# Nine mixer buffers for seven in a two-layer diffusion step, and an output projection that closes over attention

## The chip, the cores and the metric

The kernel runs on one core of a Trainium2 chip. A core has five engines with a queue of instructions each: PE (TensorE, matrix products; its weight loads are shown as PEld), DVE (VectorE), ACT (ScalarE), POOL (GpSimd) and SP (SyncE, which here only issues transfers). Each engine takes its instructions in the order in which they stand in its queue. The metric is the device time of one execution in microseconds (us).

## The reference

One inference step of a backbone with two layers of one form, each with its own weights. 128 context rows and 512 latent rows (640 in all) of width 1024 go through, per layer:

```python
hn = rmsnorm(x, norm_w[0]) * (1.0 + scale1) + shift1
z = hn @ w_in                               # 1024 -> 9 * 256
q, k, v, gb, gc, xb, xr, gr, xp = jnp.split(z, 9, axis=-1)
y_a = diff_attn(q, k, v, ...)               # 4 heads; softmax - lam * softmax, then a norm per head
y_b = gb * depthwise_conv(gc * xb, conv_b_w)
y_c = (hf + hb) * gelu(gr)                  # hf, hb: RG-LRU of conv(xr), forward and backward
y_d = pool_mixer(xp, pool_w, pool_scale)
x = x + gate1 * (concatenate([y_a, y_b, y_c, y_d]) @ w_out)
hn = rmsnorm(x, norm_w[1]) * (1.0 + scale2) + shift2
x = x + gate2 * (square(relu(hn @ w_mlp1)) @ w_mlp2)
```

The shifts, scales and gates come from a product of a conditioning vector with `w_ada`. All is float32.

## The kernel before

**Layout.** Activations lie transposed: the 1024 features are 8 chunks of 128 partitions, the 640 rows are columns, in two halves A and B of 320. To keep float32's precision, each operand is split into a high part (rounded to fp32r) and a low part (the rest), and a product is three matmuls: high x high, low x high, high x low. A result tile of 128 features by 320 columns over 8 chunks is thus a group of 24 matmuls of 320 columns. Weights come by transfers into five staging buffers `st`; ACT makes the high half `wh` (L276), DVE the low half `wl` (L259). `whl` has four buffers of each.

**Who sets the order.** The program is written down by Python generators. The main line writes the matmul groups; each call of `tick` lets every waiting helper (`rope_gen`, `attn_gen`, `rg_gen`, `gelu_gen`, `pool_gen`, `convb_gen`) write its next piece and lets the weight stream take a step. `until` calls `tick` again and again until a condition holds, a free buffer for instance. A scheduler then orders each engine's instructions by the place at which they were written down and by when their operands are there in its own model. What comes out is a fixed queue for each engine.

**The mixer stage of a layer.** The main line does `q`, `k`, then (`ORD`) `v`, `xr`, `gc`, `xb`, `xp`, `gr`, `gb`. Evacuated projections lie in the mixer buffers `m` (`NM` of them, 664 columns each, used round robin); helpers take temporaries from `z` and `m`. Output chunk pairs of the mixer are y0, y1 (attention), y2, y3 (short convolution, made from `gb`), y4, y5 (RG-LRU with gelu), y6, y7 (pooling).

- Attention unit: scores into `S` (L1022, PE), maximum (L1031, DVE), two exponentials (L1035, ACT), their combination `e` (L1042, DVE), transposes (L1049, L1054, PE), copies to `pt` (L1056, L1057, ACT), product with values (L1069, PE), copy to `osb` (L1074, DVE).
- Attention's closing, after its last unit: squares (L1110, ACT), sums per head (L1113, PE), scale `fin` (L1116 DVE, L1118 root on ACT, L1120 reciprocal on DVE); then for f = 0 and 1: spread over columns (L1131, DVE), five transposes into `TA` and `TB` (L1135, PE; one buffer each), scaled product (L1138, DVE), high part (L1139, ACT), low part (L1140, DVE). That is y0 and y1.
- RG-LRU: gates (L1177 PE, L1181 ACT), roots (L1199), products (L1202, L1203), scans (L1210), sums (L1212, L1218). Gelu and gate: L1231 to L1242, split at L866 and L868. Pooling: L1259 to L1275, product L1288 (PE), split L1290 (ACT) and L1291 (DVE). Convolution's last step: L1373 (DVE), L1376 (ACT), L1379 (DVE).

**The output projection's opening** (`gemm_early`, L799) holds four result tiles open in four PSUM banks (two of `g`, two of `S`). It first adds the chunks named in `EARLY`, then waits until all mixer outputs have been written down and no helper is left, then adds the others (`late`) and evacuates each tile into the residual (L1443, DVE). Before, the early chunks are y0, y1, y6, y4, y2, y3 (18 matmuls a tile), the late ones y5 and y7 (6 a tile). After these four tiles the projection goes on with 24 matmuls a tile (L778). Beside it run parts of the `w_ada` product on DVE and ACT (L501, L499) and the next norm's squares (L691, L694, L697).

Of the kernel before, what the change touches and what calls it, by code (L numbers as in the profile page):

```python
# [24 lines left out]
DEPTH = 2  # L25
EPS = 1e-6
GP = 664
NM = 7
OFF = 120
OFFW = 120  # L30
OFFO = 0
OFFT = 60
EARLY = (0, 1, 6, 4, 2, 3)
ORD = ("v", "xr", "gc", "xb", "xp", "gr", "gb")
QH = (0,)
BT = (1, 2)
# [82 lines left out]
class Net:  # L119
    def __init__(self, tc, es, ins, outs, consts):  # L120
# [14 lines left out]
        self.z = Slots(sl, [f"z{i}" for i in range(16)], [P, XC])  # L135
        self.m = Slots(sl, [f"m{i}" for i in range(NM)], [P, GP])
        self.e = Slots(sl, [f"e{i}" for i in range(3)], [P, T])
# [1177 lines left out]
    def layer(self, l, last):  # L1315
# [157 lines left out]

        self.gemm_early(seq[:4], mov_y, evo, EARLY, [k for k in range(KT) if k not in EARLY], gate)
        self.gemm(seq[4:], mov_y, evo,
# [399 lines left out]
```

## Time and profile before

| | |
|---|---|
| time, median of 3 runs | 1445.24 us (1445.22 to 1445.91) |
| the profiled execution | 1442.92 us, its span 1441.1 us |
| PE busy | 1416.9 us, 98% of the span |
| DVE, ACT, POOL busy | 1028.0, 728.4, 61.9 us |
| mean granted clock of PE | 0.994 |

Busy time of PE counts the matmuls' modelled ends, which overlap: a 320-column matmul is listed with 0.31 us, while the next starts 0.147 us later. Start times say more there. On DVE and ACT too, the next instruction starts a little before the listed end of the one before it.

### The profile page before, as it was taken

The numbers are of one execution on the slowest core, as the hardware profiler recorded it, in microseconds if no ns is written. First come the engines' busy times: TensorE is split into PE (matmuls) and PEld (weight loads), VectorE is DVE, ScalarE is ACT, GpSimd is POOL, SyncE is SP. The second block draws the span as 40 slices with busy tenths as digits, with TensorE's granted clock in tenths as the row PEclk, the third lists the DMA queues.
The fourth block names the chain that finished last, engine by engine and source line by source line (L and its number), as shares of the span: only waits on it lengthen the run. The fifth ranks groups of instructions, "written<-read, shape, count | busy, mean of one in ns | idle before, by whom it ended". The sixth has DMA issues, their size and how long they took to land.

```text
span 1441.1 us, 24506 instructions
## 1 busy us (share of the span) xinstructions
PE 1416.9 (98%) x9703; PEld 1345.6 (93%) x9703; DVE 1028.0 (71%) x1938; ACT 728.4 (51%) x1377; POOL 61.9 (4%) x105
## 2 busy tenths in 40 slices
PE   7999999999999999999999999999999999999998
PEld 6877989999999999999999999999999999999997
DVE  4566889896968769588968778998384644644753
ACT  5534795365347237237445577636532722722731
POOL 1122000010000000000102200000000000000000
PEclk8999999999999999999999999999999999999999
DMA  9686214435245635446634401262232432432401
GB/s 330 204 223 182 81 35 94 158 118 178 90 146 176 190 114 170 156 148 199 197 102 129 129 30 59 45 191 74 88 102 76 145 103 77 143 103 79 142 15 73
DMA packets 154970, 183.45 MB, mean 127 GB/s; under 512 B 10788, under 2 KB 130040, under 8 KB 154856
## 3 DMA queue, kind: packets, MB, share of 16 engines
q1 hardware_dynamic: 150264, 175.29, 39.7%
q0 software_dynamic: 4224, 6.45, 2.0%
q8 instruction: 76, 1.25, 0.4%
q14 instruction: 38, 0.31, 0.1%
q10 hardware_dynamic: 368, 0.16, 0.0%
HBM read 169.28 MB, written 3.15 MB: 120 GB/s over the span
## 4 chain that ended last, share of the span: by engine, by line
PE 82%; DVE 8%; DMA 6%; ACT 2%; issue 1%; POOL 0%; DVEq 0%; ACTq 0%
PE g_L_0A L778 9%; PE g_L_1A L778 9%; PE g_L_1B L778 9%; PE g_L_0B L778 9%; PE S L443 9%; PE f L443 5%; DMA st<-in_w_mlp 2%; DMA st<-in_w_ada 2%; PE g_L_v L1405 2%; PE g_L_o_0B L778 1%; PE g_L_o_1B L778 1%; PE g_L_o_1A L778 1%; PE g_L_o_0A L778 1%; PE TB L443 1%; PE TB L1069 1%; DVE wl L259 1%
## 5 line engine op out<-in xcount | busy, mean ns | idle before, releaser
L259 DVE TENSOR_TENSOR wl<-st,wh 128x1024 fp32r<-128x1024 f32 x212 | 258.3, 1221 | 104.1 <-ACT wh L321 55.4
L276 ACT CAST wh<-st 128x1024 fp32r<-128x1024 f32 x132 | 138.4, 1049 | 126.7 <-PE g_L_1B L778 85.0
L321 ACT CAST wh<-st 128x1024 fp32r<-128x1024 f32 x84 | 88.1, 1049 | 136.1 <-PE g_L_1B L778 94.9
L778 PE MATMUL g_L_0A<-z,wh 128*128 128x320 f32 (+1 forms) x512 | 124.2, 315 | 0.0
L778 PE MATMUL g_L_1A<-z,wh 128*128 128x320 f32 (+1 forms) x512 | 121.6, 314 | 0.0
L778 PE MATMUL g_L_0B<-z,wh 128*128 128x320 f32 (+1 forms) x512 | 116.5, 307 | 0.0
L778 PE MATMUL g_L_1B<-z,wh 128*128 128x320 f32 (+1 forms) x512 | 116.2, 307 | 0.0
L778 PEld LDWEIGHTS g_L_0A<-z,wh 128*128 128x128 f32 x512 | 88.2, 188 | 2.2 <-ACT z L418 2.0
L778 PEld LDWEIGHTS g_L_1A<-z,wh 128*128 128x128 f32 x512 | 87.6, 188 | 0.8 <-issue 0.8
L778 PEld LDWEIGHTS g_L_0B<-z,wh 128*128 128x128 f32 x512 | 86.2, 188 | 1.7 <-DVE x L1443 1.7
L778 PEld LDWEIGHTS g_L_1B<-z,wh 128*128 128x128 f32 x512 | 86.4, 188 | 0.9 <-issue 0.8
L501 DVE SCALAR_TENSOR_TENSOR pt<-st,SC,pt 128x512 f32<-128x512 f32 x112 | 79.7, 744 | 10.1 <-ACT pt L499 5.4
L501 DVE SCALAR_TENSOR_TENSOR m<-st,SC,m 128x512 f32<-128x512 f32 x112 | 78.8, 744 | 7.4 <-DMA st<-in_w_ada 5.5
L778 PE MATMUL g_L_0A<-z,wl 128*128 128x320 f32 (+1 forms) x256 | 79.9, 312 | 0.0
L778 PE MATMUL g_L_1A<-z,wl 128*128 128x320 f32 (+1 forms) x256 | 79.8, 312 | 0.0
L778 PE MATMUL g_L_1B<-z,wl 128*128 128x320 f32 (+1 forms) x256 | 78.6, 307 | 0.0
L778 PE MATMUL g_L_0B<-z,wl 128*128 128x320 f32 (+1 forms) x256 | 78.3, 306 | 0.0
L694 ACT ACTIVATE e<-x 128x320 f32<-128x320 f32 (+2 forms) x56 | 26.3, 470 | 102.8 <-DVE x L1443 102.7
L318 DVE TENSOR_TENSOR st<-st,st 128x1024 f32<-128x1024 f32 x48 | 58.5, 1220 | 27.0 <-DMA st<-in_w_mlp 26.9
L443 PE MATMUL S<-hh,wh 128*128 128x320 f32 x192 | 61.8, 322 | 3.6 <-DVE e L461 3.2
L1031 DVE TENSOR_REDUCE mx<-S 128x2 f32<-128x1280 f32 x32 | 47.5, 1486 | 20.2 <-PE S L1022 20.0
L443 PE MATMUL S<-hh,wl 128*128 128x320 f32 x192 | 59.3, 309 | 0.0
(682 smaller groups left out, 4205.5 us busy)
## 6 DMA issues: line engine op xcount, KB each, us to landing
st<-in_w_mlp SPq DMA_DIRECT2D x164, 512.0 KB
st<-in_w_ada SPq DMA_DIRECT2D x80, 512.0 KB
st<-in_w_in SPq DMA_DIRECT2D x36, 512.0 KB
st<-in_w_out SPq DMA_DIRECT2D x16, 512.0 KB
z<-in_w_ada SPq DMA_DIRECT2D x24, 256.0 KB
z<-qk SPq DMA_DIRECT2D x32, 80.0 KB
z<-qk POOLq DMA_DIRECT2D x32, 80.0 KB, 4.0
xt<-in_x_sample SPq DMA_DIRECT2D x4, 512.0 KB
```

Of the source, the lines that this page charges most:

```text
L259: eng.tensor_tensor(wl.rearrange("p k c -> p (k c)"), st, wh.bitcast(F32).rearrange("p k c -> p (k c)"), OP.subtract)
L276: nc.scalar.copy(wh.rearrange("p k c -> p (k c)"), st)
L318: nc.vector.tensor_tensor(st, st, self.held[add][0], OP.add)
L321: nc.scalar.copy(wh.rearrange("p k c -> p (k c)"), st)
L443: nc.tensor.matmul(bank[mi][:, 0:HC], w[:, k, sl], x, start=(fresh and n == 0), stop=(n == 11), skip_group_check=not fresh)
L501: nc.vector.scalar_tensor_tensor(acc[:, 0:512], w, col, acc[:, 0:512], OP.mult, OP.add)
L694: nc.scalar.activation(s[:, 0:n], self.x[:, k, cs], AF.Square)
L778: nc.tensor.matmul(pt[:, 0:ncols], w[:, k % 4, sl], r, start=(n == 0), stop=(n == 23))
L1031: nc.vector.tensor_reduce(mx[:, 0:2], ps[:, 128:1408].rearrange("p (s k) -> p s k", s=2), AX.X, OP.max)
L1069: nc.tensor.matmul(tb[64 * j:64 * j + 64, 0:P], self.vsb[:, kt, (h - 1 + j) * 64:(h + j) * 64], self.pTs[j][:, kt * P:(kt + 1) * P], start ...
L1405: nc.tensor.matmul(pt[:, 0:256], a[:, k, ts], b[:, k % 4, :], start=(n == 0), stop=(n == 23))
```

## The change

Three constants. `NM`: nine buffers `m0` to `m8` for seven. `EARLY`: four chunks for six, in another order; the late ones are now y0, y1 (attention), y5 and y7, so the four tiles have 12 early and 12 late matmuls each. The scratch in which POOL's transfers are prepared shrinks from 8192 to 4096 bytes per partition.

```diff
-NM = 7
+NM = 9
...
-EARLY = (0, 1, 6, 4, 2, 3)
+EARLY = (2, 6, 4, 3)
...
-    nc = bacc.Bacc("TRN2", target_bir_lowering=False, num_devices=1, dynamic_dma_scratch_size=8192)
+    nc = bacc.Bacc("TRN2", target_bir_lowering=False, num_devices=1, dynamic_dma_scratch_size=4096)
```

Every engine has the same instructions as before. Their order differs in two stretches, one per layer: from about the `gc`/`xb` groups to the first tiles of the output projection. Outside of them it is the same but for a handful of swaps.

On PE in layer 0, before, the second group of attention's closing transposes (`TA_2536`, of `e_49`) stands among the matmuls of `gb`:

```order
L778 MATMUL g_L_gb_0B<-hh,wh_2211 128x320
L1135 MATMUL TA_2536<-cst,e_49_2538 128x128 x4
L1135 MATMUL TB_2537<-cst,e_49_2538 128x128
L778 MATMUL g_L_gb_0B<-hh,wl_2212 128x320
L778 MATMUL g_L_gb_0B<-hl,wh_2211 128x320
L778 MATMUL g_L_gb_0B<-hh,wh_2211 128x320
```

After the change, on PE in layer 0, both groups stand behind the last early matmul of the fourth bank (on `z_60`, the low part of y3), and the matmuls on y0 (`z_63`) follow at once:

```order
L799 MATMUL S_2565<-z_59_2445,wl_2306 128x320
L799 MATMUL S_2565<-z_60_2446,wh_2305 128x320
L1135 MATMUL TA_2651<-cst,e_48_2653 128x128 x4
L1135 MATMUL TB_2652<-cst,e_48_2653 128x128
L1135 MATMUL TA_2672<-cst,e_49_2674 128x128 x4
L1135 MATMUL TB_2673<-cst,e_49_2674 128x128
L799 MATMUL g_L_e_2566<-z_63_2649,wh_2305 128x320
L799 MATMUL g_L_e_2566<-z_63_2649,wl_2306 128x320
```

Attention's closing has moved from within `gb` to behind all of the early matmuls, and its two halves have come together.

On DVE in layer 0, before, the closing from the first spread (L1131) to the second:

```order
L1131 COPY e_47_2473<-fin 128x640
L1218 TENSOR_TENSOR z_50_2059<-z_50_2059,z_53_2229 128x128
L1261 TENSOR_TENSOR m_38_2484<-m_37_2483 128x661
L1379 TENSOR_TENSOR z_58_2462<-m_25_1412,z_57_2461 128x320
L1138 SCALAR_TENSOR_TENSOR e_47_2473<-osb_102,small_107,TA_2471 128x512
L1138 SCALAR_TENSOR_TENSOR e_47_2473<-osb_102,small_107,TB_2472 128x128
L868 TENSOR_TENSOR z_62_2487<-m_35_2256,z_61_2486 128x640
L1373 TENSOR_TENSOR m_28_1476<-g_L_gb_1A,m_28_1476 128x320
L1140 TENSOR_TENSOR z_60_2470<-e_47_2473,z_59_2469 128x512
```

After the change, on DVE in layer 0, from the first spread to the first low part:

```order
L1131 COPY e_48_2653<-fin 128x640
L1131 COPY e_49_2674<-fin 128x640
L501 SCALAR_TENSOR_TENSOR pt_25_2709<-st_1932,SC,pt_25_2709 128x512
L1238 SCALAR_TENSOR_TENSOR m_37_2197<-e_47_2647,m_37_2197 128x640
L501 SCALAR_TENSOR_TENSOR pt_24_2708<-st_2097,SC,pt_24_2708 128x512
L1242 SCALAR_TENSOR_TENSOR m_37_2197<-z_49_2110,m_37_2197 128x512
L1138 SCALAR_TENSOR_TENSOR e_48_2653<-osb_102,small_107,TA_2651 128x512
L1138 SCALAR_TENSOR_TENSOR e_48_2653<-osb_102,small_107,TB_2652 128x128
L1242 SCALAR_TENSOR_TENSOR m_37_2197<-z_49_2110,m_37_2197 128x128
L501 SCALAR_TENSOR_TENSOR pt_25_2709<-st_2097,SC,pt_25_2709 128x512
L1140 TENSOR_TENSOR z_64_2650<-e_48_2653,z_63_2649 128x512
L1140 TENSOR_TENSOR z_64_2650<-e_48_2653,z_63_2649 128x128
```

Two L501 of the `w_ada` product and two gelu steps now stand between the spread and the scaled product.

On DVE in layer 1, before, the low halves of the next weights of the output projection (`wl_10236`, `wl_10251`) stand ahead of the residual of the first bank:

```order
L501 SCALAR_TENSOR_TENSOR pt_63_10204<-st_9661,SC,pt_63_10204 128x512
L259 TENSOR_TENSOR wl_10236<-st_9711,wh_10235 128x1024
L259 TENSOR_TENSOR wl_10251<-st_9918,wh_10250 128x1024
L501 SCALAR_TENSOR_TENSOR pt_62_10203<-st_9980,SC,pt_62_10203 128x512
L1443 SCALAR_TENSOR_TENSOR x<-g_L_e_10117,mod_92,x 128x320
L1443 SCALAR_TENSOR_TENSOR x<-g_L_e_10118,mod_92,x 128x320
```

After the change, on DVE in layer 1, the first of the two (`wl_10230`) stands behind the residual of the fourth:

```order
L1443 SCALAR_TENSOR_TENSOR x<-g_L_e_10036,mod_92,x 128x320
L1443 SCALAR_TENSOR_TENSOR x<-g_L_e_10037,mod_92,x 128x320
L1443 SCALAR_TENSOR_TENSOR x<-S_10035,mod_92,x 128x192
L1443 SCALAR_TENSOR_TENSOR x<-S_10035,mod_92,x 128x128
L697 TENSOR_TENSOR m_112_10171<-m_112_10171,e_184_10210 128x320
L501 SCALAR_TENSOR_TENSOR pt_63_10186<-st_9569,SC,pt_63_10186 128x512
L501 SCALAR_TENSOR_TENSOR pt_62_10185<-st_9569,SC,pt_62_10185 128x512
L501 SCALAR_TENSOR_TENSOR pt_63_10186<-st_9569,SC,pt_63_10186 128x512
L1443 SCALAR_TENSOR_TENSOR x<-S_10035,mod_92,x 128x192
L1443 SCALAR_TENSOR_TENSOR x<-S_10035,mod_92,x 128x128
L259 TENSOR_TENSOR wl_10230<-st_9623,wh_10229 128x1024
```

The weights' low half has moved behind the evacuation of all four early banks.

## Rows read from the trace of the kernel before

**Rows 1.** The page's engines: busy us, share of the span, instructions.

```profile
PE 1416.9 (98%) x9703; PEld 1345.6 (93%) x9703; DVE 1028.0 (71%) x1938; ACT 728.4 (51%) x1377; POOL 61.9 (4%) x105
```

**Rows 2.** Windows of changed stretches: length, engines' busy us, granted clock, DMA share, GB/s.

```profile
137.00:232.80 95.80, 95.08 (x683) 86.05 (x682) 83.54 (x164) 75.47 (x144) 0.81 (x1) 1.00 0.27 67
232.80:250.50 17.70, 17.70 (x119) 17.38 (x118) 17.15 (x36) 7.47 (x15) 1.21 (x2) 1.00 0.38 122
834.00:926.90 92.90, 91.50 (x671) 84.74 (x671) 80.53 (x158) 70.38 (x136) 0.81 (x1) 1.00 0.20 46
926.90:945.00 18.10, 18.10 (x122) 17.78 (x121) 17.53 (x37) 8.31 (x15) 0.00 (x0) 1.00 0.37 117
```

**Rows 3.** What PE waited for: us in total, times, the longest.

```profile
PE S L1022 <- DMA out_new_cache_v<-vsb: 2.4, 1, 2.4
PE TA L1049 <- DVE e L1042: 1.5, 4, 0.9
PE TA L1135 <- DVE e L1138: 0.2, 1, 0.2
```

**Rows 4.** PE, timeline of layer 0: start, us, instruction, count.

```profile
217.03 1.17 PE L1113 MATMUL TB<-hsel,e 128*128 128x2 f32 x10
222.69 0.60 PE L1135 MATMUL TA<-cst,e 128*128 128x128 f32 x4
236.20 0.70 PE L1288 MATMUL U<-m,plw 128*128 128x320 f32 x2
239.20 0.31 PE L799 MATMUL S<-z,wh 128*128 128x320 f32 x1
239.35 0.31 PE L799 MATMUL S<-z,wl 128*128 128x320 f32 x1
```

**Rows 5.** ACT, timeline of layer 0; in brackets the idle time before.

```profile
211.11 0.53 ACT L1290 ACTIVATE z<-U,PT 128x320 fp32r<-128x320 f32 x1 [1.04 <-PE U L1288]
...
214.51 0.71 ACT L499 ACTIVATE pt<-st,SC 128x512 f32<-128x512 f32 x1
215.15 0.74 ACT L1110 ACTIVATE e<-osb 128x640 f32<-128x640 f32 x1
...
229.70 0.62 ACT L1139 CAST z<-e 128x512 fp32r<-128x512 f32 x1 [0.32 <-DVE e L1138]
...
232.92 1.05 ACT L276 CAST wh<-st 128x1024 fp32r<-128x1024 f32 x1
233.87 0.54 ACT L1376 CAST z<-m 128x192 fp32r<-128x192 f32 x2
```

**Rows 6.** DVE, timeline of layer 0.

```profile
207.99 1.27 DVE L1210 TENSOR_TENSOR_SCAN z<-z,PT,z 128x512 f32<-128x512 f32 x1
221.68 0.81 DVE L1131 COPY e<-fin 128x640 f32<-128x640 f32 x1
223.77 0.74 DVE L1138 SCALAR_TENSOR_TENSOR e<-osb,small,TA 128x512 f32<-128x512 f32 x1
224.43 0.34 DVE L1138 SCALAR_TENSOR_TENSOR e<-osb,small,TB 128x128 f32<-128x128 f32 x1
225.82 0.68 DVE L1140 TENSOR_TENSOR z<-e,z 128x512 fp32r<-128x512 f32 x1
234.07 0.82 DVE L1238 SCALAR_TENSOR_TENSOR m<-e,m 128x640 f32<-128x640 f32 x1
236.20 0.88 DVE L1242 SCALAR_TENSOR_TENSOR m<-z,m 128x512 f32<-128x512 f32 x2
240.14 2.73 DVE L501 SCALAR_TENSOR_TENSOR pt<-st,SC,pt 128x512 f32<-128x512 f32 x4
242.79 2.35 DVE L259 TENSOR_TENSOR wl<-st,wh 128x1024 fp32r<-128x1024 f32 x2
247.35 0.68 DVE L1443 SCALAR_TENSOR_TENSOR x<-S,mod,x 128x192 f32<-128x192 f32 x2
```

**Rows 7.** Window behind PE's wait of 2.4 us: columns as in rows 2.

```profile
92.90:96.30 3.40, 3.40 (x13) 3.40 (x14) 0.00 (x0) 0.00 (x0) 0.00 (x0) 0.50 0.51 129
```

## The prediction

> **What bounds the kernel now.** I read the page's engine table first: PE (TensorE) is busy 1416.9 of 1441.1 us [rows 1]. So an edit moves the time by what it does to PE's queue and nearly by nothing else. PE takes its instructions in the order in which they stand: when one waits, all behind it wait, matmuls with their operands ready among them.
>
> The change moves instructions in two stretches only, one per layer: from the convolution's and the RG-LRU's matmuls to the first blocks of the output projection. Next I read the table by stage [rows 2]. From 137.0 to 232.8 us (layer 0) PE is idle for 0.72 us, from 834.0 to 926.9 us (layer 1) for 1.40 us. In the opening of the output projection (17.70 and 18.10 us) it is not idle at all. The whole that waiting costs PE where the order changes is thus 2.1 us; a better order has no more than that to win from waits. The list of what PE waits for gives the causes [rows 3]: the softmax operand `e` from DVE (1.5 us over the whole run), and once the second transposes of attention's closing, 0.2 us. The 2.4 us for a DMA lie at 90 us, ahead of the first changed instruction.
>
> A rule of the Trainium skill speaks for the buffers: "Perfetto Trace Analysis", under "Identifying Performance Opportunities", says that a gap which repeats on the engine that should be saturated can mean that buffers are too few. No PE wait here ends with a mixer buffer's release [rows 3]; by the rule the change would win those 2.1 us and cost nothing.
>
> **The change part by part.** *Two more mixer buffers.* No instruction is added or removed on any engine; SP's order stays. What alters is the pace. With seven buffers the program, while it was written down, often had to go round waiting for a free one, and attention's and the mixers' helpers moved on by a step each time; with nine they move one step per twelve matmuls. So attention's last unit, which ended in `gr`/the start of `gb`, now ends with `gb`, and its closing (L1110 to L1140) has moved from under the 96 matmuls of `gb` to the place where nothing but the output projection is left.
>
> *EARLY with four outputs for six.* Before the late outputs, PE has 4 x 12 = 48 matmuls of the projection to do instead of 72. At 0.147 us from one start to the next [rows 4] that is 7.1 us of cover instead of 10.6. The order shows what follows them: both groups of transposes (L1135) side by side, then the matmuls on attention's outputs. TA is one buffer, so the second group must wait until DVE has read the first (L1138), and each later matmul waits for a cast on ACT (L1139) or a subtraction on DVE (L1140). Before, `gb` matmuls stood between these links. I follow the links by durations of the same operations, counting from one start to the next where rows follow each other.
>
> Layer 0, zero at the end of `gb_1B`. PE: one pool matmul 0.70, 12 matmuls 1.76, L1113 1.17, 36 matmuls 5.3: 8.9 [rows 4]. ACT meanwhile: L276 (its buffer is freed at zero) 0.95, L499, L1110, L499 0.64 each, L276 0.95, the L1376 pair 0.54: 4.4, the pool's L1290 0.45 more [rows 5]. DVE's L1291 waits for that, and L1116 stands behind it: 5.5. The root on ACT, one 640-wide operation, the reciprocal, one L501 (0.67) and L1131 (0.75) bring DVE to 8.1 [rows 6]. The first transposes need not wait; PE ends them at 9.6 (five of 0.15 [rows 4]). Now DVE has five operations ahead of L1138, as the order shows: L1131 0.75, L501 0.67, L1238 0.75, L501 0.67, L1242 0.6; with L1138 itself, 0.66, it is 12.2. **PE waits 2.65 us.** The second transposes end at 13.0, six matmuls at 13.9. Then L1138 0.26, the rest of L1242 0.2, L501 0.67 and L1140 0.61 give the first low half at 13.95; three matmuls, 14.4. The rest of L1140 0.2, the second L1138 0.66 and the cast 0.6 give 15.4: PE waits 1.0. Six matmuls, 16.3; L1138 0.26, one 640-wide operation and L1140: 16.4. Waits in sum **3.9 us**.
>
> Layer 1, zero at the end of the last L1069. PE: 12 matmuls, a pool matmul, 12 matmuls, L1113: 5.4; 24 matmuls: 8.9. DVE: a small copy 0.2, a pair of halves 0.5, two 640-wide operations 1.5, a scan 1.2 [rows 6], two pieces 0.8, a 640-wide one 0.75; then L1116, which needs L1113, at 5.5; a scan, the reciprocal, the rest of scans and sums 1.2 and L1131: 8.9. First transposes done at 9.6. DVE: L1233 0.4, L1131, L1234, L1138: 11.4, a wait of 1.8. Second transposes to 12.1, six matmuls to 13.0. DVE: L1138 0.26, L501 0.67, L1138 0.66, L1238 0.75, L1140 0.61: 14.3, a wait of 1.3. Seven matmuls, 15.3; L1140 0.2, L1242 0.8, L1140 0.61: 15.95, a wait of 0.65. From here 37 matmuls (5.4 us) run through: 21.4. But the next weights' low half (L259, `wl_10230`) now stands on DVE behind the residual of the fourth bank; before it stood ahead of the first. DVE reaches L1443 of the first bank after two L501 at 18.5, takes the other L1443 of banks two and three and L697 by 20.4, three L501 (2.0) by 22.4, the fourth bank's 0.6 by 23.0 and L259's 1.17 by 24.2 [rows 6]. PE waits 2.8. Sum **6.55 us**.
>
> Both layers: 10.4 us. Bounds: nothing, if DVE were always ahead by the few us that separate it from PE here; 15 us, if DVE comes into these stretches late by two of its scans (2.4 us) in each layer. I take 10.4, since the terms are durations of the same operations.
>
> *The clock.* Behind the wait of 2.4 us at 90 us the granted clock was 0.50 for 3.40 us [rows 7], the lower of the two levels, 1.2 GHz; PE ran half as fast, so at most 1.7 us were lost. The new waits of 2.65, 1.8 and 2.8 us are of that size. Cost 0 to 3.4 us for one such drop per layer; part would fall into times in which PE waits anyway, so I take 1.0. The Trainium skill ("TensorE: Matmul & The Clock Gate", "Why this matters for your kernels") advises against idle gaps between bursts of matmuls because the clock falls back to half; the row agrees, and by the rule alone both layers would pay, 3.4.
>
> *What is won.* The waits for `e` and for the pool's bank inside `xb` to `gr` should go, since attention no longer runs as fast as DVE lets it: of the 2.1 us I take 1.5 (bounds 0 and 2.1). Small matmuls stand in 77 runs among the large ones instead of 85; a run costs about 0.1 to 0.3 us at its edges (transposes of 0.15 us each against 0.147 for a large one, yet 0.70 for a lone pool matmul in two passes), so 0.7 (bounds 0 and 2.4).
>
> *Half the transfer scratch.* POOL's transfers are the same and in the same order but for one pair. Bounds: nothing, and at worst one more wait like the 2.4 us one per layer, 4.8. I take nothing.
>
> Sum: 10.4 + 1.0 - 1.5 - 0.7 = +9.2 us. The profiled execution took 1442.92 us, 2.3 less than the median 1445.24 of the timed runs; the difference is added to that median: **1454.4 us**.
>
> **Rivals.** *The closing is hidden after all (faster).* If DVE and ACT go through the links several us earlier than I count, so that the chain from L1113 to L1140 ends within the 5.3 us of early matmuls, only the gains remain: up to -2.1 - 2.4 = -4.5, likely -2: 1443. It decides at the second transposes: they would have to be free to start at 9.6 and not at 12.2. For it: DVE is not busy all the time (83.5 of 95.8 us in layer 0 [rows 2]). Against it: five operations in a fixed order ahead of L1138, two of them for work nobody waits for. Chance 0.10.
>
> *All waits of now go, and two thirds of the closing are hidden (no change).* 2.1 + 0.7 won, 3 lost: within 0.2% of the time before, 2.9 us, about what a measurement of this kernel can tell. Chance 0.06.
>
> *DVE arrives late and the clock falls in both layers (much slower).* 15 + 3.4 - 1 = +17: 1462. DVE is busy for 17.15 of 17.70 us in the opening [rows 2]; what comes late there is not caught up. Chance 0.14.
>
> *The change does not do what it says, the smaller scratch stalls POOL's copies for the stacks:* +4.8 on top, 1459, with a new PE wait for `S` at L1022. Chance 0.03.
>
> *Forecast:* the closing is exposed in both layers, +4 to +13. Chance 0.67.
>
> Faster by over 0.2%: 0.08 (part of the first rival). Within 0.2%: 0.09. Slower by over 0.2%: 0.83. For 8 in 10 I leave out the lower half of the first two rivals and the upper half of the third: 1446 to 1462; the forecast's own range is 1449 to 1458.
>
> **What the new profile would show.** PE's list of waits with L1135 for DVE's L1138 (2.65 and 1.8 us), L799 for ACT's L1139 and DVE's L1140 (1 to 1.3 us), and in layer 1 L778 for DVE's L259 (2.8 us). A granted clock under 1.00 near 250 or 950 us. No more L1049 waits on `e` between 137 and 927 us. If the openings show PE busy throughout, as now, the forecast is wrong, and the time will be 1443 or so. If L1135 waits but L259 does not, 2.8 us of it are wrong.

## The result and the profile after

The changed kernel took 1456.45 us (median of 6 runs, 1452.73 to 1458.29), the kernel before 1445.68 us beside it (6 runs, 1445.22 to 1447.07): a ratio of 1.0067, 95% interval 1.0057 to 1.0077. That is slower by 0.67%, 2 us above the forecast of 1454.4 and inside its range. The profiled execution took 1457.38 us, its span 1455.6 us.

The page's engine line after, answering to [rows 1], shows what is not the cause: instruction counts are the same and DVE's and ACT's work is too. PE is listed with 7.8 us more, though it does the same: the span holds 31.7 us at a granted clock of 0.50 for 17.1 before, in which a matmul takes longer.

```profile
PE 1424.7 (98%) x9703; PEld 1351.7 (93%) x9703; DVE 1031.2 (71%) x1938; ACT 730.5 (50%) x1377; POOL 61.9 (4%) x105
```

The windows of the two openings in [rows 2], asked of the profile after (PE, PEld, DVE, ACT, POOL busy, granted clock, DMA share, GB/s). PE was never idle in them before; now they hold 1.64 and 1.85 us of idle PE, and the second has a clock of 0.91. They are cut at the times of before, and the changed kernel comes there 3 and 6 us later, so the second one ends ahead of the last waits:

```profile
232.80:250.50 17.70, 16.06 (x111) 15.02 (x110) 17.02 (x37) 7.34 (x14) 1.99 (x3) 1.00 0.21 27
926.90:945.00 18.10, 16.25 (x114) 15.10 (x113) 16.22 (x33) 10.04 (x17) 0.81 (x1) 0.91 0.02 1
```

The list of what PE waited for, after, beside [rows 3]. All places that the prediction named are there, and three that it did not: L707, `S` at L799 on L1443, and 0.4 us at L778 for `wh` of `xb` (its line stands below, in the run with the ticks put back). The waits at L1049, which were to go, are still there.

```profile
PE S L1022 <- DMA z<-qk: 4.2, 1, 4.2
...
PE g_L_o_0A L778 <- DVE wl L259: 2.1, 1, 2.1
PE TA L1135 <- DVE e L1138: 1.6, 2, 0.8
...
PE g_L_e L799 <- DVE z L1140: 1.4, 2, 1.1
PE TB L707 <- DVE m L697: 1.3, 1, 1.3
...
PE TA L1049 <- DVE e L1042: 0.9, 2, 0.7
PE g_L_e L799 <- ACT z L1139: 0.8, 1, 0.8
...
PE S L799 <- DVE x L1443: 0.5, 1, 0.5
```

Where the time went is read from the starts of the same instructions. From L1177's first matmul to L716's first in a layer the kernel before took 142.85 us (layer 0) and 154.10 us (layer 1), the changed one 145.86 and 163.01: **+3.0 and +8.9 us**, 11.9 in sum. Between and behind these stretches the two executions differ by less than 1 us in all. Ahead of the first they differ by 3.3 us, of which more below. The same two stretches as windows:

```profile
142.21:288.07 145.86, 143.35 (x1003) 133.00 (x1003) 127.92 (x243) 94.63 (x173) 1.99 (x3) 1.00 0.32 93
828.59:991.60 163.01, 156.24 (x1090) 145.96 (x1089) 129.43 (x245) 96.22 (x182) 0.83 (x2) 0.98 0.24 72
```

PE is idle in them for 2.51 and 6.77 us, and before it was for 0.73 and 1.40. So layer 1's 8.9 us are 5.4 of idle time and 3.4 lost in two windows at half clock (below). Layer 0's 3.0 us are 1.8 of idle time and 1.2 in which PE was busy longer at the full clock. No run shows what these 1.2 come from.

PE's closing in layer 0, after, beside [rows 4]: the second transposes wait for the first group's L1138, the fourth late operand for ACT's L1139.

```profile
235.62 2.29 PE L1113 MATMUL TB<-hsel,e 128*128 128x2 f32 x20
...
243.15 0.60 PE L1135 MATMUL TA<-cst,e 128*128 128x128 f32 x4
...
244.71 0.65 PE L1135 MATMUL TA<-cst,e 128*128 128x128 f32 x4 [0.85 <-DVE e L1138]
...
247.94 0.42 PE L799 MATMUL g_L_e<-z,wh 128*128 128x320 f32 x1 [0.80 <-ACT z L1139]
```

DVE in the same place, beside [rows 6]: between the spreads (L1131) and the first product (L1138) stand two L501, L1238 and most of L1242, as the order said.

```profile
237.95 0.18 DVE L1116 SCALAR_TENSOR_TENSOR fin<-fin,TB 128x20 f32<-128x20 f32 x1 [0.68 <-PE TB L1113]
...
239.80 1.54 DVE L1131 COPY e<-fin 128x640 f32<-128x640 f32 x2
241.25 0.74 DVE L501 SCALAR_TENSOR_TENSOR pt<-st,SC,pt 128x512 f32<-128x512 f32 x1
241.91 0.82 DVE L1238 SCALAR_TENSOR_TENSOR m<-e,m 128x640 f32<-128x640 f32 x1
242.65 0.75 DVE L501 SCALAR_TENSOR_TENSOR pt<-st,SC,pt 128x512 f32<-128x512 f32 x1
243.31 0.68 DVE L1242 SCALAR_TENSOR_TENSOR m<-z,m 128x512 f32<-128x512 f32 x1
243.91 0.74 DVE L1138 SCALAR_TENSOR_TENSOR e<-osb,small,TA 128x512 f32<-128x512 f32 x1
```

PE in layer 1, after: the waits for the closing, for L259, and at the next norm (L707).

```profile
941.48 0.66 PE L1135 MATMUL TA<-cst,e 128*128 128x128 f32 x4 [0.73 <-DVE e L1138]
...
944.39 0.56 PE L799 MATMUL g_L_e<-z,wh 128*128 128x320 f32 x2 [1.12 <-DVE z L1140]
...
946.01 0.57 PE L799 MATMUL g_L_e<-z,wh 128*128 128x320 f32 x2 [0.32 <-DVE z L1140]
...
954.52 0.41 PE L778 MATMUL g_L_o_0A<-z,wl 128*128 128x320 f32 x1 [2.08 <-DVE wl L259]
...
985.77 0.83 PE L707 MATMUL TB<-ones,m 128*128 128x1 f32 x6 [1.33 <-DVE m L697]
```

DVE in layer 1, behind the closing: L259 for the block that PE wants next (L778) is reached after three L501 and the last bank's residual.

```profile
950.67 2.07 DVE L501 SCALAR_TENSOR_TENSOR pt<-st,SC,pt 128x512 f32<-128x512 f32 x3
952.66 0.67 DVE L1443 SCALAR_TENSOR_TENSOR x<-S,mod,x 128x192 f32<-128x192 f32 x2
953.25 1.22 DVE L259 TENSOR_TENSOR wl<-st,wh 128x1024 fp32r<-128x1024 f32 x1
```

The wait at L707 hangs on the last residual (L1443) ahead of the norm, through ACT's L694 and DVE's L697. Before, DVE stood idle until PE had ended that tile; after, DVE was busy with two L501 and came to it 1.1 us behind PE. The first line is from the profile before, the others from the one after:

```profile
970.58 0.55 DVE L1443 SCALAR_TENSOR_TENSOR x<-g_L_o_1A,mod,x 128x320 f32<-128x320 f32 x1 [1.57 <-PE g_L_o_1A L778]
...
982.47 1.41 DVE L501 SCALAR_TENSOR_TENSOR m<-st,SC,m 128x512 f32<-128x512 f32 x2
983.80 0.55 DVE L1443 SCALAR_TENSOR_TENSOR x<-g_L_o_1A,mod,x 128x320 f32<-128x320 f32 x1
```

Two windows of layer 1, columns as above, beside [rows 7]: 3.42 us each at a clock of 0.50 (1.2 GHz), with PE busy throughout.

```profile
935.82:939.24 3.42, 3.42 (x15) 3.42 (x14) 3.42 (x9) 0.98 (x1) 0.81 (x1) 0.50 0.00 0
987.02:990.44 3.42, 3.42 (x18) 2.32 (x17) 0.95 (x4) 0.09 (x1) 0.00 (x0) 0.50 0.00 0
```

### The profile page after: what moved, and what is told of

Its sections match the earlier page's. It is cut to its first block, busy times and chain, and to the rows that moved or that the text cites. A ratio compares the mean times of both kernels' runs of the same rounds, so it can differ in the third digit from the quotient of the medians.

```text
span 1455.6 us, 24495 instructions
## 1 busy us (share of the span) xinstructions
PE 1424.7 (98%) x9703; PEld 1351.7 (93%) x9703; DVE 1031.2 (71%) x1938; ACT 730.5 (50%) x1377; POOL 61.9 (4%) x105
## 4 chain that ended last, share of the span: by engine, by line
PE 82%; DVE 8%; DMA 6%; ACT 2%; issue 1%; SPq 0%; DVEq 0%; ACTq 0%
PE g_L_0A L778 9%; PE g_L_1A L778 9%; PE S L443 9%; PE g_L_1B L778 9%; PE g_L_0B L778 9%; PE f L443 5%; DMA st<-in_w_ada 2%; PE g_L_v L1405 2%; DMA st<-in_w_mlp 2%; DVE wl L259 2%; DVE pt L501 1%; PE TB L443 1%; PE TB L1069 1%; PE S L1022 1%; PE g_L_o_1B L778 1%
## 5 line engine op out<-in xcount | busy, mean ns | idle before, releaser
L259 DVE TENSOR_TENSOR wl<-st,wh 128x1024 fp32r<-128x1024 f32 x212 | 258.7, 1223 | 103.9 <-ACT wh L321 55.1
L778 PE MATMUL g_L_0A<-z,wh 128*128 128x320 f32 (+1 forms) x512 | 124.0, 315 | 0.0
L778 PE MATMUL g_L_1A<-z,wh 128*128 128x320 f32 (+1 forms) x512 | 121.5, 313 | 0.0
L778 PE MATMUL g_L_0B<-z,wh 128*128 128x320 f32 (+1 forms) x512 | 116.3, 307 | 0.0
L778 PE MATMUL g_L_1B<-z,wh 128*128 128x320 f32 (+1 forms) x512 | 116.2, 307 | 0.0
L778 PEld LDWEIGHTS g_L_0A<-z,wh 128*128 128x128 f32 x512 | 88.2, 188 | 2.2 <-ACT z L418 2.0
L778 PEld LDWEIGHTS g_L_1A<-z,wh 128*128 128x128 f32 x512 | 87.6, 188 | 0.8 <-issue 0.8
L778 PEld LDWEIGHTS g_L_0B<-z,wh 128*128 128x128 f32 x512 | 86.2, 188 | 1.7 <-DVE x L1443 1.7
L778 PEld LDWEIGHTS g_L_1B<-z,wh 128*128 128x128 f32 x512 | 86.4, 189 | 0.9 <-issue 0.8
L501 DVE SCALAR_TENSOR_TENSOR pt<-st,SC,pt 128x512 f32<-128x512 f32 x112 | 79.6, 748 | 8.4 <-ACT pt L499 4.7
L501 DVE SCALAR_TENSOR_TENSOR m<-st,SC,m 128x512 f32<-128x512 f32 x112 | 78.9, 746 | 8.1 <-DMA st<-in_w_ada 5.4
L694 ACT ACTIVATE e<-x 128x320 f32<-128x320 f32 (+2 forms) x56 | 26.4, 471 | 108.0 <-DVE x L1443 107.9
L778 PE MATMUL g_L_1A<-z,wl 128*128 128x320 f32 (+1 forms) x256 | 79.8, 312 | 0.0
L778 PE MATMUL g_L_0A<-z,wl 128*128 128x320 f32 (+1 forms) x256 | 79.8, 312 | 0.0
L778 PE MATMUL g_L_1B<-z,wl 128*128 128x320 f32 (+1 forms) x256 | 78.6, 307 | 0.0
L778 PE MATMUL g_L_0B<-z,wl 128*128 128x320 f32 (+1 forms) x256 | 78.3, 306 | 0.0
L443 PE MATMUL S<-hl,wh 128*128 128x320 f32 x192 | 59.3, 309 | 0.0
```

The lines of the kernel that those rows point to most:

```text
L259: eng.tensor_tensor(wl.rearrange("p k c -> p (k c)"), st, wh.bitcast(F32).rearrange("p k c -> p (k c)"), OP.subtract)
L443: nc.tensor.matmul(bank[mi][:, 0:HC], w[:, k, sl], x, start=(fresh and n == 0), stop=(n == 11), skip_group_check=not fresh)
L501: nc.vector.scalar_tensor_tensor(acc[:, 0:512], w, col, acc[:, 0:512], OP.mult, OP.add)
L694: nc.scalar.activation(s[:, 0:n], self.x[:, k, cs], AF.Square)
L778: nc.tensor.matmul(pt[:, 0:ncols], w[:, k % 4, sl], r, start=(n == 0), stop=(n == 23))
```

## The experiments

Each kernel was timed in five rounds beside the kernel before; groups of three or four shared a chip. A run of the kernel before on those chips took 1440.7 to 1450.9 us, a wider spread than in the first comparison, so the stretches in the profiles (time added per layer, taken as above; one execution each) stand beside the ratios.

| kernel | median us | ratio to before (95%) | layer 0, layer 1 |
|---|---|---|---|
| changed, first | 1456.45 | 1.0057 to 1.0077 | +3.0, +8.9 |
| changed, again | 1456.03 | 1.0052 to 1.0089 | +4.4, +9.3 |
| before, small scratch | 1444.94 | 0.9977 to 1.0007 | 0.0, +1.1 (clock at 0.50 once, from 914 us) |
| before, new EARLY | 1445.48 | 0.9987 to 1.0013 | 0.0, 0.0 |
| changed, old EARLY | 1463.15 | 1.0100 to 1.0142 | +8.9, +10.7 |
| changed, closing first | 1454.02 | 1.0040 to 1.0079 | +1.8, +7.1 |
| changed, ticks put back | 1447.14 | 0.9999 to 1.0028 | +1.4, 0.0 |
| the same, helpers only | 1448.40 | 1.0008 to 1.0032 | +1.4, 0.0 |
| changed, half the ticks | 1445.55 | 0.9987 to 1.0015 | +0.3, -1.2 |
| changed, one L259 earlier | 1452.04 | 1.0032 to 1.0061 | +2.8, +8.2 |
| the same, again | 1453.34 | 1.0038 to 1.0074 | +3.7, +7.0 |
| changed, fewer L501 | 1460.92 | 1.0091 to 1.0130 | +12.0, +4.4 |

### The three constants, one at a time

**The scratch alone.**

```diff
-    nc = bacc.Bacc("TRN2", target_bir_lowering=False, num_devices=1, dynamic_dma_scratch_size=8192)
+    nc = bacc.Bacc("TRN2", target_bir_lowering=False, num_devices=1, dynamic_dma_scratch_size=4096)
```

> The kernel before with one edit: the scratch of POOL's transfers at 4096 bytes for 8192. The order on every engine is that of before. Theory A (scratch costs nothing; the longer wait of 4.2 us for S at L1022 in the changed kernel, against 2.4 us before, is chance): the time of before, 1445.7 within 1.5 us, the wait at L1022 2 to 3 us, POOL's copies of 80 KB at about 6.7 us from issue to landing. Theory B (the smaller scratch holds POOL's copies back): the wait at L1022 is 4.2 us again, the copies take 8.3 us as in the changed kernel, and the time is 1.8 to 3 us above before, 1447.5 to 1448.7.

Ratio 0.9992. POOL's 80 KB copies took 6.4 us in the median from issue to landing (before 6.7), and the wait at L1022 was shorter than before:

```profile
PE S L1022 <- DMA out_new_cache_v<-vsb: 1.9, 1, 1.9
```

Theory A holds. Over all profiles this wait lay between 1.9 and 4.2 us; with the full scratch it was 2.4 and 2.6 us, with half of it anything in that range, 2.4 in the changed kernel's second profile. So the smaller scratch does not fix the 4.2 us; this wait differs from run to run, and why was not tried.

**EARLY alone, on seven buffers.**

```diff
-EARLY = (0, 1, 6, 4, 2, 3)
+EARLY = (2, 6, 4, 3)
```

> The kernel before with one edit: EARLY = (2, 6, 4, 3), seven mixer buffers and the scratch kept. In the order, attention's closing stays among the matmuls of gb, since the pace is that of seven buffers. Theory A (the buffers' pace moves the closing, EARLY alone only takes cover that is not needed here): 1445.7 within 2 us, no wait at L1135 above 0.3 us, at most 0.9 us at L799 for y3, which is asked for 0.9 us earlier. Theory B (EARLY exposes the closing by itself, 48 matmuls being too few): waits at L799 or L1135 of 2 us or more per layer, 1450 to 1454.

Ratio 1.0000, and both stretches took the time of before to within 0.05 us. The only waits of PE there from 200 to 262 us and from 900 to 960 us are three that stood in the list of before too: 0.3 us at L1288, 0.9 at L1049 and 0.2 at L1135.

Theory A: with the closing under `gb`, y0 and y1 are there when the projection begins, and it does not matter which chunks come last.

**Nine buffers with the old EARLY.**

```diff
-EARLY = (2, 6, 4, 3)
+EARLY = (0, 1, 6, 4, 2, 3)
```

> The changed kernel with EARLY as before, (0, 1, 6, 4, 2, 3): nine mixer buffers and the small scratch. In the order, both groups of transposes now stand right behind L1113, with no early matmul of the projection ahead of them. Theory A (the buffers' pace moves the closing, and EARLY in its new form covers part of it): the 48 matmuls (7.1 us) that covered it per layer are gone, so PE waits 5 to 8 us more per layer at L1135 and L799 and the time is 1464 to 1472. Theory B (the change of EARLY is what costs, nine buffers alone do not): 1446 to 1449. Theory C (both matter by halves): 1450 to 1456.

1463.15 us, 6.7 above the changed kernel's 1456.45: theory A's mechanism, a little under its band of 1464 to 1472. PE reaches the closing with nothing to do (its list of waits, 200 to 1000 us, and a window with columns as above):

```profile
PE TA L1135 <- DVE e L1131: 8.7, 3, 3.8
PE g_L_e L799 <- ACT z L1139: 4.5, 3, 2.7
```

```profile
233.00:243.00 10.00, 5.04 (x20) 4.27 (x20) 9.52 (x21) 4.01 (x7) 0.79 (x1) 0.51 0.11 19
```

With the new EARLY the stretches are 5.9 and 1.8 us shorter: in layer 0 that is the size theory A gave its 48 early matmuls (5 to 8 us), in layer 1 much less. So nine buffers are what costs, and the new EARLY repays part of it.

### The pace

**The ticks put back.** While it was written down, the kernel before went round 7 times (8 in layer 1) waiting for a buffer for `xb`'s second tile and twice for `gr`'s first. The changed kernel never waits there; it goes round five times (seven in layer 1) at the opening, waiting for y0, y1 and y5. This run puts the old ticks back and keeps all three constants of the change:

```diff
-                self.until(lambda: self.m.ok(), "m slot " + name)
+                [self.tick() for _ in range({("xb", 1): 7 + l, ("gr", 0): 2}.get((name, mi), 0))]
```

> The changed kernel (nine buffers, new EARLY, small scratch) with the steps put back in which the kernel before went round waiting for a buffer: 7 ticks ahead of the second xb evacuation in layer 0, 8 in layer 1, and 2 ahead of the first gr evacuation in each. In the order, attention's transposes (L1135) stand among the matmuls of gb again. Theory A (the pace of the helpers is the whole cause, the buffers themselves cost nothing): no wait above 0.3 us at L1135 or in the opening, the time of before, 1444 to 1448. Theory B (nine buffers cost by themselves, by what their round robin makes wait): 1451 or more, with waits that stay at L778, L799 or L707.

1447.14 us, ratio 1.0013 (0.9999 to 1.0028): theory A, with most of the loss gone. L1135 does not wait, and layer 1 takes the time of before. Layer 0 keeps 1.4 us, 0.5 of them idle PE. What PE waited for from 137 to 262 us:

```profile
PE TA L1049 <- DVE e L1042: 0.6, 1, 0.6
PE g_L_xb_0A L778 <- ACT wh L276: 0.4, 1, 0.4
```

**Helpers alone.** In the added ticks the weight stream stands still:

```diff
-    def tick(self):
-        self.credit = min(self.credit, 1.0) + (self.rates[self.ii] if self.ii < len(self.rates) else 1.0)
-        while self.credit >= 1.0:
+    def tick(self, stream=1):
+        self.credit = min(self.credit, 1.0) + (self.rates[self.ii] if self.ii < len(self.rates) else 1.0) * stream
+        while stream and self.credit >= 1.0:
...
-                self.until(lambda: self.m.ok(), "m slot " + name)
+                [self.tick(0) for _ in range({("xb", 1): 7 + l, ("gr", 0): 2}.get((name, mi), 0))]
```

> As the kernel with the ticks put back, but in the added ticks only the helpers take a step and the weight stream does not. Theory A (what the nine steps do is to carry attention and the mixers forward): the time of that kernel within 1.5 us, 1444 to 1448. Theory B (it was the weight stream's steps that kept L259 and L276 early): 1449 to 1454, with waits for wl or wh at L778 in the output projection.

1448.40 us, just outside A's band, but the stretches are those of the run above (+1.4, 0.0), and no wait for `wl` or `wh` stands in the output projection. It is the helpers' steps that count. The 1.3 us between the two medians lie inside both intervals. This run's own interval (1.0008 to 1.0032) is clear of 1: a little of the loss stays with the ticks put back, the 1.4 us of layer 0 in both profiles, and its cause was not looked for.

**Half of the ticks.**

```diff
-                self.until(lambda: self.m.ok(), "m slot " + name)
+                [self.tick() for _ in range({("xb", 1): 4 + l, ("gr", 0): 1}.get((name, mi), 0))]
```

> As the kernel with the ticks put back, but about half of them: 4 ahead of the second xb evacuation in layer 0, 5 in layer 1, and 1 ahead of the first gr evacuation. In the order, the first transposes now stand right ahead of the first early matmul and the second ones six to nine matmuls on, so some 39 of the 48 early matmuls (5.7 us) lie behind them. Theory A (the closing costs only what it is longer than the work behind its start): from the second transposes to the first low half DVE needs about 3.5 us, which 5.7 us cover, so 1444 to 1448. Theory B (the chain of the closing is exposed as soon as it leaves gb, whatever lies behind it): waits of 1 us or more at L799 in each layer, 1449 to 1453.

1445.55 us, ratio 1.0001: theory A. The second transposes now start without a wait, with most of the early matmuls still behind them:

```profile
235.22 0.60 PE L1135 MATMUL TA<-cst,e 128*128 128x128 f32 x4
...
236.97 0.65 PE L1135 MATMUL TA<-cst,e 128*128 128x128 f32 x4
```

DVE ends the first low half (L1140) by 240.2 us and the second by 242.6; PE asks for neither before. So the closing need not lie inside `gb`: in layer 0 it begins 7.4 us earlier than in the changed kernel, counted from the start of the stretch, and that is enough. Of the versions with nine buffers this one has the lowest median. Its stretches are 0.9 us shorter than those of before, which the timed runs can't tell from nothing.

### What the loss is made of

**The closing preferred.** One `with` more, so L1131 stands at L1132 and L1138 to L1140 at L1139 to L1141.

```diff
+            with self.tc.high_priority(offset=CLOSE):
+                nc.vector.tensor_copy(ov, ...)
...
+            with self.tc.high_priority(offset=CLOSE):
+                for dst, src in ((slice(0, 512), ta), (slice(512, 640), tb[:, 0:P])):
```

> The changed kernel, with attention's spreads, transposes, products, high and low parts (L1131, L1135, L1138 to L1140) written down under a priority of 120 places, so that the scheduler puts them ahead of helper work: the two groups of transposes stand nine matmuls apart among the early matmuls. (One line more in the closing; L1131 stands at L1132, L1135 at L1135, L1138 to L1140 at L1139 to L1141.) Theory A (the serial closing behind other work on DVE is what costs): the waits for the closing (1.6 us at L1135, 0.8 and 1.4 us at L799) fall to under 1 us in sum, and with fewer drops of the clock the time is 1449 to 1453. Theory B (DVE is full there, so that what is preferred only pushes the rest): new waits of 3 us or more at L778 for L259 or at L707, L554 take their place, 1455 to 1459.

1454.02 us, between both theories. The waits for attention are gone entirely, and in layer 1 one wait of 4.44 us stands in their place, for y5, the other late output (0.46 us in layer 0). Its chain (L1234, L1236, L1238, L1242, L866) fell behind the closing and behind L501 (PE, ACT and DVE of layer 1; lines are one further down here):

```profile
947.00 0.64 PE L799 MATMUL g_L_e<-z,wh 128*128 128x320 f32 x1 [4.44 <-ACT z L866]
```

```profile
946.22 0.72 ACT L866 CAST z<-m 128x640 fp32r<-128x640 f32 x1 [3.33 <-DVE m L1243]
```

```profile
941.91 2.07 DVE L501 SCALAR_TENSOR_TENSOR pt<-st,SC,pt 128x512 f32<-128x512 f32 x3
943.90 0.82 DVE L1239 SCALAR_TENSOR_TENSOR m<-e,m 128x640 f32<-128x640 f32 x1
```

So the opening waits for two chains that share DVE, and to prefer one delays the other. The stretches are 3.0 us shorter in sum than the changed kernel's, and 8.9 us of the loss stay: an order within these few us does not replace an earlier start.

**One L259 earlier.** The low half of layer 1's second output block moves ahead of the first residual:

```diff
-        return OFFW if k in (...) else OFFO if k == ("o", 0) else 0
+        return OFFW if k in (...) else OFFO if k == ("o", 0) else 20 if key[0] == ("L1", "o", 1) else 0
```

> The changed kernel with one instruction written under a priority of 20 places: L259 for the first half of layer 1's second output block. In the order on DVE it stands ahead of the residual of the first bank (as before) and no longer behind that of the fourth; the closing keeps its order. Theory A (its place on DVE costs 2.1 us): the wait of L778 for it goes, the residuals come 1.2 us later with no PE wait above 0.5 us, and the time is 2 us below that of the changed kernel, 1454 to 1455; 1452 if the wait at L707 and the fall of the clock behind it go too. Theory B (DVE is full, the 1.2 us come back): new waits of 1 to 2 us at L778 or L799 on L1443 or at L707 on L697, 1455.5 to 1457.5.

1452.04 us here, the number of theory A's second case. It was run once more beside the changed kernel on one chip:

> The changed kernel once more, unaltered, beside the kernels of this call on the same chip. Theory A (its loss is fixed by the order of its instructions): 9 to 12 us over the kernel before, with the same PE waits in the profile (1.6 us at L1135, 2.2 at L799, 2.1 at L778 for L259, 1.3 at L707), while the 1.5 us more at low clock in the first 30 us and the longer wait of 4.2 us at L1022 vary. Theory B (part of the loss was that one chip's): 5 to 8 us.

> The kernel with L259 of layer 1 under a priority of 20 places once more, beside the changed kernel on the same chip. Theory A (the place of L259 is worth what the first run showed, 1452.0 us, some 4 us under the changed kernel of another chip): 3 to 5 us less than the changed kernel here. Theory B (its wait at L778 only fell from 2.1 to 1.8 us in that profile, and the rest was the other chip): 0 to 2 us less.

1453.34 against 1456.03 us: 2.7 less, between the two theories of that pair, while their intervals overlap (1.0038 to 1.0074 and 1.0052 to 1.0089). The changed kernel's loss repeats (ratio 1.0071, the named waits the same to about 0.1 us, but for L1022). But the gain did not come as expected. PE, DVE and ACT of the first of these two runs, layer 1:

```profile
936.73 0.66 PE L1135 MATMUL TA<-cst,e 128*128 128x128 f32 x4 [1.81 <-DVE e L1138]
939.64 0.56 PE L799 MATMUL g_L_e<-z,wh 128*128 128x320 f32 x2 [1.12 <-DVE z L1140]
941.25 0.57 PE L799 MATMUL g_L_e<-z,wh 128*128 128x320 f32 x2 [0.32 <-DVE z L1140]
952.38 0.44 PE L778 MATMUL g_L_o_0A<-z,wl 128*128 128x320 f32 x1 [1.82 <-DVE wl L259]
```

```profile
942.99 1.22 DVE L259 TENSOR_TENSOR wl<-st,wh 128x1024 fp32r<-128x1024 f32 x1
...
951.10 1.22 DVE L259 TENSOR_TENSOR wl<-st,wh 128x1024 fp32r<-128x1024 f32 x1
```

```profile
949.24 1.05 ACT L276 CAST wh<-st 128x1024 fp32r<-128x1024 f32 x1 [3.02 <-DMA st<-in_w_out]
```

The first half is done at 944 us, and PE now waits nearly as long for the block's second half, whose weights land at 949.2 us. What did go is the wait of 1.3 us at L707, and with it the fall of the clock behind it: neither stands at that place in the two profiles (in the first of them the clock fell at 952.62 us instead, behind the wait for the second half).

**Fewer L501.** The products of the opening, six per layer, are left out, so what they add to the conditioning is missing from the results.

```diff
-                nc.vector.scalar_tensor_tensor(acc[:, 0:512], w, col, acc[:, 0:512], OP.mult, OP.add)
+                self.quiet or nc.vector.scalar_tensor_tensor(acc[:, 0:512], w, col, acc[:, 0:512], OP.mult, OP.add)
...
-        S = self.psS.get()
+        S, self.quiet = self.psS.get(), True
...
-        self.psS.put(S)
+        self.quiet = self.psS.put(S)
```

> The changed kernel without the products L501 that the weight stream writes down while the projection's opening is being written (6 per layer of 0.69 us on DVE, 4.1 us; the conditioning of the second norm's gate and of what follows it lacks these terms). In the order, the links of the closing keep their places; in layer 0 two L259 move up ahead of and between the spreads (L1131), in layer 1 one L259 between the two L1138 and one ahead of the last L1140. Theory A (behind the closing it is DVE's backlog that costs; in the closing it is the serial chain itself): L778's wait for L259 (2.1 us) and L707's for L697 (1.3 us) go, the waits at L1135 and L799 stay at 3 to 5 us in sum, and the time is 3 to 5 us below that of the changed kernel, 1451 to 1453.5. Theory B (DVE's other work is the whole cause, of the closing's waits as well): all of them go and the time is 1446 to 1449. Theory C (the chain alone, backlog without effect): 1455 to 1457.

1460.92 us, which none of the three theories had. In layer 0 the stream ran ahead, and an L499 that waits for its transfer came to stand on ACT ahead of attention's second casts:

```profile
251.27 1.33 ACT L499 ACTIVATE m<-st,SC 128x512 f32<-128x512 f32 x2 [7.38 <-DMA st<-in_w_ada]
...
253.12 0.81 ACT L1139 CAST z<-e 128x512 fp32r<-128x512 f32 x2
```

PE waited 8.45 us for that. Layer 1 alone answers to theory A (+4.4 for +8.9 us; no wait for L259, 0.26 us at L707, 1.8 us left for the closing and 1.0 for y5), but what was taken away there was replaced by other work, so the run as a whole settles nothing.

## Why the prediction was right, point by point

**The mechanism.** "Attention's last unit [...] now ends with `gb`, and its closing has moved from under the 96 matmuls of `gb`" because nine buffers spare the ticks: shown. Putting back the ticks takes most of the loss away (1.0013, and 1.0020 with the helpers alone, for 1.0067), half of them takes away all that the timed runs can tell, and EARLY and scratch alone change nothing.

**Layer 0's closing: 3.9 us predicted, 1.65 measured** (0.85 and 0.80). The wait on L1139 was as forecast (1.0). (The four waits in the prediction's own times add up to 3.8.) The mis-sized term is the 2.65 us at the second L1135. Two steps of it were off, both in the same direction, counted as in the prediction from the end of `gb`, here 233.33 us, where the next matmul starts. PE came to the first transposes at 9.8 us, not 8.9: I counted L1113 as 1.17 us from a row of ten matmuls, but now all twenty stand together, 2.29 us. And DVE was through with the first L1138 at 11.2, not 12.2: I let L1116 stand behind ACT's L1290 until 5.5, but it came at 4.6, held only by L1113.

**Layer 1's closing: 3.75 us predicted, 2.2 measured** (0.73, 1.12, 0.32). Here the first two terms hold where the clock does not fall ahead of them: the first run with L259 moved has 1.81, 1.12 and 0.32 us for 1.8, 1.3 and 0.65; the third was half its size in both. In the changed kernel PE ran at half the clock from 935.82 us. Counted from the start of L1113 it came to the first transposes at 7.29 us, in that run at 5.83, but to the second ones at 8.73 and 8.41: of 1.5 us only 0.3 are left, because the two costs overlap.

**L259: 2.8 predicted, 2.1 measured**, in its place and for the named reason (three L501 and a residual ahead of it). That an earlier L259 would free PE was not forecast and proved false; the block's second half is next.

**Missed:** the residual of the third bank (0.5 us) and L707 (1.3 us at 985.8 us). From 963 us to the next norm DVE's residuals start 1.1 to 2.7 us behind the end of their tiles on PE (before, 1 us or less; the rows at L1443 above show the last of them), so its backlog lasts 40 us beyond the closing; the prediction stopped at the first tiles of the projection.

**The clock: 1.0 predicted.** Layer 1 had two windows at 0.50 in the first profile, each up to 1.7 us of work lost; the second profile had three, one in layer 0. By the Trainium skill ("TensorE: Matmul & The Clock Gate", "Why this matters for your kernels") idle gaps between bursts bring the clock down. The rows do not settle it here: the fall at 987 us came 1.3 us behind the wait at L707, the one at 936 us has no wait listed in the 50 us before it, and the longest of the new waits, 2.1 us at L778, brought none.

**Won: 2.2 predicted, nothing found.** The waits for `e` fell only from 1.5 to 0.9 us, and a new one of 0.4 us for `wh` came. Without its waits, layer 0's stretch up to `g_L_o_0B` got 0.75 us longer, not shorter, so the term for fewer runs of small matmuls did not show. Part of its ground was a misreading: the 0.70 us of L1288 [rows 4] is the listed length of two overlapping matmuls, and in the trace of before the next one starts 0.30 us behind the first. The Trainium skill's rule that repeating gaps may mean too few buffers ("Perfetto Trace Analysis", "Identifying Performance Opportunities") would have won these waits; with the ticks put back, nine buffers alone gave 1.0013 (0.9999 to 1.0028), so the wait list was right that no PE wait hung on a buffer.

**EARLY.** The prediction compared 7.1 us of cover with 10.6. That is the wrong reading: y0 and y1 stand first among the old six, so with the late closing those 72 matmuls could not begin before it was done. The four-chunk EARLY is the better one here, by 6.7 us in the medians and 7.7 in the stretches.

**The sum.** Closings and L259 were 4.5 us too large (10.4 against 5.9). On the other side 6.9 us were missing: up to 2.4 of clock, 1.8 for L707 and the residual, 2.7 of gains that did not come. 9.2 - 4.5 + 6.9 = 11.6, beside 11.9 in the stretches and 10.8 in the medians. The forecast came out within about 2 us because these errors nearly cancel; what it had firmly was the sign and the place.

## What to carry to other kernels

Where a program's writer waits for buffers, those waits also set how far its helpers have come: before giving it more buffers, count the rounds that it now waits, and put them back on purpose if a serial chain has to end in time. A chain of DVE, PE and ACT at a stage's end costs by when it starts, and a preferred order inside its last microseconds can move the wait to the next late operand, as it did here for most of the loss. A DVE backlog made in one stage can be collected later, here 40 us later, at the next norm.

## Not expected of the hardware

In seven profiles (fourteen layers) the twenty L1113 matmuls of two columns stand together for 2.3 us, and in eight of these layers the granted clock fell to 0.50 between 2.3 and 4.8 us after their start. In six of the eight PE had no listed wait there; the other two are the kernel with the old EARLY, where waits of 3.2 and 3.8 us follow right behind L1113. (In the changed kernel's second profile, both layers: L1113 at 230.97 and 930.88, clock at 0.50 from 234.63 and 934.36.) In the other six layers, with the same rows, it did not fall then. In the six profiles in which L1113 stands as two groups of ten, it fell so in one layer of twelve. Whether these matmuls bring it down was not tried.

The 14.5 us between the two profiled spans include 3.3 us from the first 100 us, where the order of the instructions is that of before: 17.1 us at half clock for 10.2 at the start, and the longer wait at L1022. Two profiles of these kernels are better compared by stretches than by spans.
